# Where a four-byte constant and the identity lie in on-chip memory, in a decoder layer on one core

## The chip, the core and the metric

The kernel runs on one of the eight cores of a Trainium2 chip, as one launch. A core has a matrix engine (TensorE, "PE" in the profile, with its weight loads as a row of their own, "PEld"), two engines for elementwise work (VectorE, "DVE"; ScalarE, "ACT"), GpSimd ("POOL") and SyncE ("SP"), which here only issues transfers, and 16 DMA engines. Engines compute on an on-chip memory of 128 partitions; a tile takes the same range of bytes in each partition, so its place is one byte offset. Matmul results go to a second memory, PSUM.

The metric is the device time of one execution in microseconds (us), as a median of several runs.

## The reference

One layer of a hybrid decoder on 512 tokens of 1024 channels, with one layer of weights. Cut to what is computed:

```python
u = _rmsnorm(h, norm1_g[l])
proj = u @ w_in[l]
a_glu, q, k, v, r, g_low, gate_a, gate_b = _split_cols(proj)

c = a_glu[..., :CONV_CH] * jax.nn.sigmoid(a_glu[..., CONV_CH:])
c = _causal_dwconv(c, conv_dw_w[l], conv_dw_b[l])              # 31 taps
c = jax.nn.silu(_layernorm(c, conv_ln_g[l], conv_ln_b[l]))
y_conv = c @ w_conv_out[l]

gk = jax.nn.log_sigmoid((g_low @ w_gate_up[l] + b_gate[l])) / GATE_NORMALIZER
o = _gla_chunked(qh, kh, vh, gkh)                              # 4 heads, chunks of 64
o = o * lax.rsqrt(jnp.mean(o * o, axis=-1, keepdims=True) + EPS) * gla_norm_g[l]
o = o.reshape(bsz, seq, GLA_VDIM) * jax.nn.silu(r)
y_gla = o @ w_gla_out[l]

merged = jax.nn.sigmoid(gate_a) * y_conv + jax.nn.sigmoid(gate_b) * y_gla
h = h + merged @ w_o[l]

u2 = _rmsnorm(h, norm2_g[l])
z = _causal_dwconv(u2 @ w_ffn_up[l], ffn_dw_w[l], ffn_dw_b[l])  # 3 taps
h = h + (jax.nn.silu(z[..., :FFN_DIM]) * z[..., FFN_DIM:]) @ w_ffn_down[l]
return _rmsnorm(h, final_g)
```

## The kernel before

**Products.** Each fp32 matrix is held as two parts in the type fp32r, a high part (a rounded copy, made by ScalarE) and a low part (the rest, made by VectorE or by a transfer that adds). A product is three matmuls into one PSUM bank: low x high, high x low, high x high. That is `mm3` (lines 554, 555 and 556), and nearly all matmuls of the trace carry these lines. A matmul names a stationary operand, which a weight load brings into the array, and a moving operand of 512 or 256 columns. Some large products are done with seven block products in the place of eight, for which sums of blocks are made first; these have 256 columns, or 512.

**Stages.** In order of time: normalisation and the value projection; the GLU, the convolution's taps on VectorE and the attention's heads beside the input projection; the output gate's projection w_r (about 255 to 280 us), the merge gates with w_gla and w_conv (to about 427 us), w_o with the second norm, and four groups of up-projection and down-projection. Weights are loaded by SyncE's queue into `raw`, split into `whi` and `wlo`, four buffers each, a few tiles ahead of their use.

**What meets in a matmul.** Activations of the input and up-projection are in `u` (uh, ul). In w_conv the stationary operand is whi or wlo and the moving one `ch` (high part) or `c` (low part). In w_r the stationary operand is a slice of u or of sums of it (`hq` in the heap, `sumsq` in the pool late), and the moving one whi or wlo. In the merge gates sums of u move (`hq`, `sumsq`, `c`), in the up-projection `xq`, `usq`, `gainq` and `btmpq`, 256 columns wide. In a row of the profile "mm<-ch,wlo" names the bank and the two operands.

**Places.** Tiles are given places in the order in which they are made, each padded to 32 bytes. Pools made on the left begin at the low end, one behind the other: const, weights, acts, temps, then heap and conv (later ffn). Pools made with "right" come from the high end: edge, and over time gla, late, r, conv_hi, residual. Ahead of const lie 1,024 bytes for descriptors and four small constants of 32 bytes. Three pads in `PADS` shift what comes behind them. The offsets in the compiled program before:

| tile | offset in bytes | modulo 512 |
|---|---|---|
| (pad of 416) | 1,152 | 128 |
| ident, the 128x128 identity for transposes | 1,568 | 32 |
| pp, per-channel parameters | 2,080 | 32 |
| ones, mhalf | 3,904 and 4,416 | 320 |
| eps, four bytes, the bias of one square root in the layer norm (`ln_var`) | 4,448 | 352 |
| shares, run64, keep | 4,480, 4,992, 6,016 | 384 |
| gains | 6,144 | 0 |
| raw, whi, wlo (four each) | from 6,176 on | 32 |
| u (uh, ul; also sums) | from 55,328 on | 32 |
| gain, x and what shares their buffers (gainq, xq, oa) | from 88,096 on | 32 |
| tmp, btmp (also btmpq) | from 107,680 on | 160 |
| heap (h, hq), conv (c), ffn (usq and others) | from 124,704 on | 288 |
| right side: ch, r, sumsq, hres, rx, gate_up, att, q, k, state | from 199,680 on | 0 |

Of the kernel before, what the change touches and what calls it, by code (L numbers as in the profile page):

```python
# [10 lines left out]
F32 = mybir.dt.float32  # L11
# [7 lines left out]
P = 128  # L19
# [35 lines left out]
WARM = (6, 1)  # L55
MID = 4
EARLY = 2
PADS = (416, 992, 768)
ET = mybir.EngineType
SEVEN = {"w_o": KT // 2, "w_down": FT // 2, "w_r": KT // 2}  # L60

# [40 lines left out]
def trunk_layer(ctx: ExitStack, tc: tile.TileContext, a: dict, out: bass.AP):  # L102
    nc = tc.nc

    def pool(name, bufs, space=None):
        kw = {"space": space} if space is not None else {}
        return ctx.enter_context(tc.tile_pool(name=name, bufs=bufs, **kw))
# [7 lines left out]
    cp = pool("const", 1)  # L115
# [13 lines left out]
    def nm(s):  # L129
        return f"{s}_{next(names)}"  # L130
# [30 lines left out]
    for i, part in enumerate((cp, edge)):  # L161
        part.tile([P, PADS[i] // 4], F32, name=nm("pad"))


    ident = cp.tile([P, P], F32, name="ident")
    make_identity(nc, ident)
    pp = cp.tile([P, PP_N], F32, name="pp")
    gate_up = gp.tile([P, HEADS * DK], F32R, name="gate_up")
    ones = cp.tile([P, P], F32, name="ones")
    mhalf = cp.tile([P, NT], F32, name="mhalf")  # L170
    eps = cp.tile([P, 1], F32, name="eps")
    shares = cp.tile([P, P], F32R, name="shares")
    run64 = cp.tile([P, T], BF16, name="run64")
    keep = cp.tile([P, P], U8, name="keep")
# [2 lines left out]
    def load_consts():  # L177
        tc.keep_in_program_order(nc.sync.dma_start(pp, a["pp"]))
        nc.gpsimd.memset(shares.bitcast(F32), -1.0 / D)
        nc.gpsimd.memset(run64, 1.0)  # L180
        nc.gpsimd.memset(run64[:, 0:T:64], 0.0)

        kf = tmp(P)
        nc.gpsimd.memset(kf, 1.0)
        nc.gpsimd.affine_select(
            kf, kf, pattern=[[1, P]], compare_op=ALU.is_ge, fill=0.0, base=0, channel_multiplier=-1
        )
        nc.gpsimd.tensor_copy(keep, kf)
        nc.gpsimd.memset(att, 0.0)
# [661 lines left out]
    start.__exit__(None, None, None)  # L851
    tp.tile([P, PADS[2] // 4], F32, name=nm("pad"))
    load_consts()
# [1205 lines left out]
```

## Time and profile before

| | |
|---|---|
| median of 3 runs | 815.84 us (815.72 to 816.29) |
| profiled execution | 815.9 us |
| its span, first to last instruction | 814.2 us |
| granted TensorE clock, mean | 0.999 |
| busy: ScalarE, GpSimd | 494.9 us (61%), 188.5 us (23%) |
| moved by DMA | 115.71 MB, mean 142 GB/s |

The profile is of one execution. "Busy" is the time in which an engine has an instruction under way; as matmuls overlap and their ends are modelled, a row's duration is longer than the distance from one matmul to the next, which is read from the starts in the timeline. A row of groups gives line, engine, operation, result<-operands, shape, count, busy time, mean ns, and the idle time ahead of it. The chain of work is followed back from the last instruction to what released each step.

### The profile page before, as it was taken

How to read it: one execution, taken by the hardware profiler on the slowest of the kernel's cores; microseconds unless marked ns; L12 is line 12 of the kernel's file. 1: busy time of each engine (PE TensorE's matmuls, PEld its weight loads, DVE VectorE, ACT ScalarE, POOL GpSimd, SP SyncE). 2: the span in 40 equal slices, each digit the busy share in tenths (PEclk: the TensorE clock that was granted, in tenths of full speed). 3: DMA queues.
4: the chain of work that ended last, by engine and by line, in shares of the span. 5: the costliest groups of instructions: out<-in, count | busy, mean ns of one | idle time of the engine just before them, and what ended most of it. 6: DMA issues, size and time to landing. Idle time of an engine off the chain costs nothing.

```text
span 814.2 us, 11423 instructions
## 1 busy us (share of the span) xinstructions
PE 806.4 (99%) x4185; PEld 689.9 (85%) x4185; DVE 708.0 (87%) x1120; ACT 494.9 (61%) x761; POOL 188.5 (23%) x166
## 2 busy tenths in 40 slices
PE   9999999999999999999999999999999999999997
PEld 7888888788888798989888898898889988899885
DVE  6779999998998898786679899979966999789996
ACT  6667788677556785593434655556445563466655
POOL 2025433332204222022001100320133310612010
PEclk9999999999999999999999999999999999999999
DMA  9488858745832443432458513146632446334662
GB/s 334 150 195 174 197 159 173 164 114 129 197 85 83 148 125 104 146 113 96 164 126 205 187 60 122 52 155 156 148 128 87 141 118 167 106 104 158 178 130 105
DMA packets 41385, 115.71 MB, mean 142 GB/s; under 512 B 7960, under 2 KB 13216, under 8 KB 41328
## 3 DMA queue, kind: packets, MB, share of 16 engines
q1 hardware_dynamic: 33968, 89.01, 32.0%
q0 software_dynamic: 7200, 25.69, 18.2%
q8 instruction: 33, 0.54, 0.3%
q14 instruction: 24, 0.20, 0.1%
q10 hardware_dynamic: 160, 0.27, 0.1%
HBM read 110.76 MB, written 3.15 MB: 140 GB/s over the span
## 4 chain that ended last, share of the span: by engine, by line
PE 84%; DVE 14%; issue 1%; ACT 1%; DVEq 0%; ACTq 0%
PE mm L554 20%; PE mm L555 20%; PE mm L556 20%; DVE c L916 5%; PE cv L555 4%; PE cv L554 4%; PE cv L556 4%; DVE aside L916 3%; PE ax L556 2%; PE ax L555 2%; PE ax L554 2%; PE mm L772 1%; PE ax L1232 1%; PE ax L1234 1%; DVE wlo L437 1%
## 5 line engine op out<-in xcount | busy, mean ns | idle before, releaser
L554 PE MATMUL mm<-uh,wlo 128*128 128x512 f32 (+1 forms) x532 | 193.8, 364 | 0.3 <-DVE wlo L477 0.3
L555 PE MATMUL mm<-ul,whi 128*128 128x512 f32 (+1 forms) x532 | 191.6, 360 | 0.0
L556 PE MATMUL mm<-uh,whi 128*128 128x512 f32 (+1 forms) x532 | 191.5, 360 | 0.0
L437 DVE TENSOR_TENSOR wlo<-raw,whi 128x1024 fp32r<-128x1024 f32 x82 | 97.8, 1198 | 29.6 <-ACT whi L435 25.9
L405 POOL TENSOR_TENSOR raw<-raw,raw 128x512 f32<-128x512 f32 x39 | 60.6, 1554 | 241.0 <-DVE wlo L437 134.3
L554 PEld LDWEIGHTS mm<-uh,wlo 128*128 128x128 f32 x532 | 100.5, 189 | 15.8 <-DVE wlo L477 0.7
L556 PEld LDWEIGHTS mm<-uh,whi 128*128 128x128 f32 x532 | 100.4, 189 | 15.4
L555 PEld LDWEIGHTS mm<-ul,whi 128*128 128x128 f32 x532 | 100.5, 189 | 14.7
L435 ACT CAST whi<-raw 128x1024 fp32r<-128x1024 f32 x82 | 78.9, 965 | 36.9 <-PE mm L556 15.1
L468 ACT CAST whi<-raw 128x1024 fp32r<-128x1024 f32 x80 | 83.5, 1047 | 27.5 <-PE mm L556 13.1
L477 DVE TENSOR_TENSOR wlo<-raw,whi 128x1024 fp32r<-128x1024 f32 x50 | 64.7, 1299 | 7.2 <-ACT whi L468 7.1
L435 ACT CAST whi<-kept 128x1024 fp32r<-128x1024 f32 (+1 forms) x40 | 40.1, 1008 | 33.7 <-DVE kept L381 17.5
L437 DVE TENSOR_TENSOR wlo<-kept,whi 128x1024 fp32r<-128x1024 f32 (+1 forms) x40 | 48.3, 1211 | 5.5 <-ACT whi L435 5.4
L916 DVE SCALAR_TENSOR_TENSOR aside<-cv,pp,aside 128x255 f32<-128x255 f32 (+6 forms) x112 | 52.0, 465 | 0.0
L916 DVE SCALAR_TENSOR_TENSOR c<-aside,btmp,c 128x247 f32<-128x247 f32 (+13 forms) x93 | 52.0, 565 | 0.0
L916 DVE SCALAR_TENSOR_TENSOR c<-cv,pp,c 128x247 f32<-128x247 f32 (+13 forms) x93 | 43.1, 463 | 1.4 <-ACT c L912 1.4
L470 ACT ACTIVATE wlo<-raw 128x1024 fp32r<-128x1024 f32 x28 | 29.4, 1059 | 19.1 <-PE mm L554 19.1
L1770 DVE SCALAR_TENSOR_TENSOR tmp<-mm,pp,tmp 128x511 f32<-128x511 f32 (+1 forms) x42 | 31.2, 742 | 3.5 <-ACT tmp L1767 3.5
L1388 ACT COPY tmp<-mm 128x256 f32<-128x256 f32 x38 | 14.0, 368 | 30.3 <-PE mm L556 29.7
L1541 DVE TENSOR_TENSOR hres<-hres,mm 128x512 f32<-128x512 f32 (+1 forms) x37 | 24.6, 674 | 4.3 <-PE mm L556 2.5
L1770 DVE SCALAR_TENSOR_TENSOR tmp<-tmp,pp,tmp 128x511 f32<-128x511 f32 (+1 forms) x32 | 27.8, 888 | 0.4
L555 PE MATMUL cv<-ul,whi 128*128 128x512 f32 (+1 forms) x72 | 25.6, 356 | 0.0
(517 smaller groups left out, 2087.8 us busy)
## 6 DMA issues: line engine op xcount, KB each, us to landing
raw<-in_w_up_dram SPq DMA_DIRECT2D x44, 512.0 KB, 3.3
raw<-in_w_glu_dram SPq DMA_DIRECT2D x16, 512.0 KB, 4.9
raw<-in_w_down_dram SPq DMA_DIRECT2D x16, 512.0 KB, 4.5
wlo<-in_w_glu_dram POOLq DMA_DIRECT2D x12, 512.0 KB, 7.1
kept<-in_w_down_dram POOLq DMA_DIRECT2D x9, 512.0 KB, 5.3
raw<-in_w_v_dram SPq DMA_DIRECT2D x8, 512.0 KB, 6.4
raw<-in_w_qk_dram SPq DMA_DIRECT2D x8, 512.0 KB, 6.1
raw<-in_w_gb_dram SPq DMA_DIRECT2D x8, 512.0 KB, 4.4
```

Source lines behind the costliest of these rows:

```text
L405: work = nc.gpsimd.tensor_tensor(out, x, y, ALU.add)
L435: nc.scalar.copy(hi, raw)
L437: two_low[:] = [nc.vector.tensor_tensor(lo, raw, hi.bitcast(F32), ALU.subtract)]
L468: nc.scalar.copy(hi, raw)
L470: pace[0] = nc.scalar.mul(lo, raw, -1.0)
L477: pace[0] = nc.vector.tensor_tensor(lo, raw, hi.bitcast(F32), ALU.subtract)
L554: nc.tensor.matmul(acc, ll, rh, start=first, stop=False, **kw)
L555: nc.tensor.matmul(acc, lh, rl, start=False, stop=False, **kw)
L556: nc.tensor.matmul(acc, lh, rh, start=False, stop=last, **kw)
L916: nc.vector.scalar_tensor_tensor(out[:, j:], x[:, : half_t - j], w, out[:, j:], ALU.mult, ALU.add)
L1541: done = nc.vector.tensor_tensor(hres[t, n][:, c], hres[t, n][:, c], acc[:, c], op)
L1770: nc.vector.scalar_tensor_tensor(z[:, s:], acc[:, : T - s], w[j], z[:, s:], ALU.mult, ALU.add)
```

## The change

The pad at the head of const is 384 bytes instead of 416, and eps is made directly behind ident instead of behind mhalf:

```diff
-PADS = (416, 992, 768)
+PADS = (384, 992, 768)
...
     ident = cp.tile([P, P], F32, name="ident")
+    eps = cp.tile([P, 1], F32, name="eps")
     make_identity(nc, ident)
     pp = cp.tile([P, PP_N], F32, name="pp")
     gate_up = gp.tile([P, HEADS * DK], F32R, name="gate_up")
     ones = cp.tile([P, P], F32, name="ones")
     mhalf = cp.tile([P, NT], F32, name="mhalf")
-    eps = cp.tile([P, 1], F32, name="eps")
     shares = cp.tile([P, P], F32R, name="shares")
```

By the rule of places, ident goes to 1,536, a multiple of 512, and eps to 2,048, with its 32 bytes up to 2,080; pp, ones and mhalf stay. As no 32 bytes are taken behind mhalf any more, shares and every left-side tile behind it lie 32 bytes lower: where they would lie without eps. The right side stays. The instruction that fills eps stays where it was in the program.

## The prediction

> **What bounds the kernel now.** I read the page first, then busy time by stretches, then the chain of work that ended last, and then, because the change moves nothing but places in memory, the timeline of TensorE with an eye on which places its operands have. The page:
>
> ```profile
> span 814.2 us, 11423 instructions
> ...
> PE 806.4 (99%) x4185; PEld 689.9 (85%) x4185; DVE 708.0 (87%) x1120; ACT 494.9 (61%) x761; POOL 188.5 (23%) x166
> ```
>
> TensorE is busy for 806.4 of 814.2 us. The weight loads (PEld, 689.9 us) run beside the matmuls, so both read the on-chip memory at the same time. Two stretches that matter below, with their columns in the order PE, PEld, DVE, ACT, POOL, granted clock, DMA share, GB/s:
>
> ```profile
> 32.00:132.00 100.00, 99.75 (x441) 82.24 (x440) 90.31 (x203) 77.23 (x121) 35.16 (x33) 1.00 0.76 186
> 360.00:424.00 64.00, 64.00 (x359) 55.53 (x358) 45.93 (x64) 31.05 (x47) 9.01 (x7) 1.00 0.43 128
> ```
>
> The clock is granted in full, and from 360 to 424 us TensorE has no gap at all while VectorE rests for 18 of 64 us. The chain of work there:
>
> ```profile
> by line: PE mm L555 24.9%; PE mm L556 24.8%; PE mm L554 24.8%; PE cv L554 8.6%; PE cv L556 8.6%; PE cv L555 8.6%
> ```
>
> It is TensorE alone: whatever a matmul of this stretch gets shorter by, the kernel gets shorter by. A busy TensorE does not say how fast it goes, though. For that I take the start of one matmul to the start of the next from the timeline. First the input projection, where the moving operand (u) and the stationary one (whi, wlo) both lie 32 bytes past a multiple of 512:
>
> ```profile
> 90.00 0.39 PE L554 MATMUL mm<-uh,wlo 128*128 128x512 f32 x1
> ...
> 91.36 0.39 PE L554 MATMUL mm<-uh,wlo 128*128 128x512 f32 x1
> ```
>
> Six matmuls in 1.36 us are 226.7 ns each. Now the convolution's output projection, w_conv. Its weights lie at 32 as before, but its activations lie at 0 (ch, on the right side of memory) and at 288 (c), all modulo 512:
>
> ```profile
> 408.44 0.40 PE L554 MATMUL mm<-ch,wlo 128*128 128x512 f32 x1
> ...
> 410.54 0.40 PE L554 MATMUL mm<-ch,wlo 128*128 128x512 f32 x1
> ```
>
> Nine matmuls in 2.10 us are 233.3 ns each, 6.6 ns more for the same shape. The output gate's projection, w_r, has the roles turned round: its stationary tiles (sumsq, right side) lie at 0 and its moving weights at 32.
>
> ```profile
> 268.01 0.39 PE L554 MATMUL mm<-whi,sumsq 128*128 128x512 f32 x1
> ...
> 272.21 0.39 PE L554 MATMUL mm<-whi,sumsq 128*128 128x512 f32 x1
> ```
>
> Eighteen in 4.20 us are 233.3 ns again. So before the change there are two paces for one shape, and the slow one stands where left-side and right-side tiles meet in a matmul.
>
> **The change part by part.** It adds, removes and reorders no instruction, wait or transfer; every queue issues the same list. It moves ident from 32 to 0 and eps from behind mhalf to behind ident. Since eps no longer takes 32 bytes behind mhalf, every left-side tile made after it (the constants shares, run64, keep and gains, all weights, activations, temporaries, heap) lies 32 bytes lower. The right side (hres, r, ch, sumsq, q, k, state, att) and pp, ones and mhalf stay. Modulo 512, weights and u go from 32 to 0, heap and c from 288 to 256, tmp and btmp from 160 to 128. The differences among left-side tiles stay; those between left and right change by 32, and w_conv and w_r come to the differences 0 and 256. The trace has a fast case for both: u against whi above (0), and a heap tile at 288 against weights at 32 (256):
>
> ```profile
> 306.06 0.39 PE L554 MATMUL mm<-h,wlo 128*128 128x512 f32 x1
> ...
> 307.42 0.39 PE L554 MATMUL mm<-h,wlo 128*128 128x512 f32 x1
> ```
>
> Six in 1.36 us, 226.7 ns. **First term, w_conv.** Two of the rows of the tile ch (counts, then min/median/max of one in ns; the two banks are mm and cv):
>
> ```profile
> L556 PE MATMUL mm<-ch,whi x48: 390/397/397, 365.2 to 426.4; 128*128 128x512 f32 x48
> L554 PE MATMUL cv<-ch,wlo x16: 392/396/400, 376.1 to 403.5; 128*128 128x512 f32 x16
> ```
>
> 48 and 16 in every product, and three products (L554, L555 with c, L556): 192 matmuls x 6.6 ns = 1.27 us, all on the chain.
>
> **Second term, w_r.** The 18 matmuls up to 272.2 us lie on the chain: 18 x 6.6 ns = 0.12 us. Behind them the chain leaves TensorE; one of its pieces is
>
> ```profile
> 275.84 0.68 DVE r L1598
> ```
>
> Up to about 288 us it runs over ScalarE and VectorE. The further 34 matmuls at this pace (0.22 us) I cost at nothing, as those engines are then what is late; 0.22 us is the other end.
>
> **Third term, 256 columns: a small loss.** Here unlike places are not slower. Both operands at 32:
>
> ```profile
> 482.02 0.28 PE L554 MATMUL mm<-uh,wlo 128*128 128x256 f32 x1
> ...
> 485.26 0.28 PE L554 MATMUL mm<-uh,wlo 128*128 128x256 f32 x1
> ```
>
> The moving operand at 0, the weights at 32:
>
> ```profile
> 374.63 0.28 PE L554 MATMUL mm<-sumsq,wlo 128*128 128x256 f32 x1
> ...
> 376.05 0.39 PE L554 MATMUL cv<-ch,wlo 128*128 128x512 f32 x1
> ```
>
> The moving operand at 160 (and in every third matmul usq, at 288), the weights at 32:
>
> ```profile
> 554.62 0.28 PE L554 MATMUL mm<-btmpq,wlo 128*128 128x256 f32 x1
> ...
> 555.33 0.28 PE L554 MATMUL mm<-btmpq,wlo 128*128 128x256 f32 x1
> ```
>
> 27 in 3.24 us are 120.0 ns, 12 in 1.42 us are 118.3, and 6 in 0.71 us are 118.3. The rows of the tile sumsq count 100 such matmuls, 28 in each of the two largest groups, the rest in groups of 12 and 8:
>
> ```profile
> L554 PE MATMUL mm<-sumsq,wlo x28: 280/282/364, 292.4 to 396.9; 128*128 128x256 f32 x28
> L556 PE MATMUL mm<-sumsq,whi x28: 276/282/285, 292.7 to 397.1; 128*128 128x256 f32 x28
> ```
>
> They go to 120.0: 100 x 1.7 ns = 0.17 us lost. btmp keeps its difference of 128 and its pace. That row also says what the fast state hangs on: 160 and 32 differ by a multiple of 64 and still do not run at 120.0, while 288 and 32 do. So I take the difference modulo 256 as what counts.
>
> **What costs nothing.** VectorE takes the same for a result on the right side (sums, offset 0) as for one on the left (c, 288); the groups by shape:
>
> ```profile
> L1682 DVE TENSOR_TENSOR sums<-tmp,sums 128x512 fp32r<-128x512 f32 x8 | 5.4, 688 | 0.0
> L1053 DVE TENSOR_TENSOR c<-ax,c 128x512 f32<-128x512 f32 x8 | 5.3, 683 | 0.0
> ```
>
> A transfer of w_r takes 6.6 us from issue to landing in a tile at 32 (raw) and 5.7 us in one at 0 (rx):
>
> ```profile
> raw<-in_w_r_dram SPq DMA_DIRECT2D x6, 512.0 KB, 6.6
> ```
>
> ```profile
> rx<-in_w_r_dram SPq DMA_DIRECT2D x1, 512.0 KB, 5.7
> ```
>
> The second is a single transfer, and the chain of the stretch above holds no DMA. I take nothing; a gain could show only in the first 32 us, and I leave 0.3 us for it. The plain fp32 matmuls of the attention run alike with 288 against 0 (h, att) and with both operands at 0 (state, q):
>
> ```profile
> L1232 PE MATMUL ax<-h,att x32: 378/379/483, 154.4 to 239.9; 128*128 128x256 f32 x32
> ```
>
> ```profile
> L1234 PE MATMUL ax<-state,q x24: 379/379/483, 155.5 to 240.3; 128*128 128x256 f32 x24
> ```
>
> 379 ns each. So ident's move should not be felt by the transposes, which are plain fp32 too.
>
> **Sum:** 1.27 + 0.12 - 0.17 = 1.22 us. The profiled execution took 815.9 us around its span of 814.2; the median shown is 815.84, so the two stand within 0.1 us. 815.9 - 1.2 = 814.7, or 814.6 from the median. I forecast **814.6**. Its own range is 814.1 (all of w_r counts, no loss, a little from the start) to 815.2 (half of it is given back to VectorE later).
>
> [...]
>
> **The rivals.** *Nothing changes* (815.9): the slow pace belongs to the right side's tiles themselves, high in memory, and not to a difference of places. For it: ch and sumsq are both up there. Against it: btmpq lies in the middle of the left side and leaves the pace of 120.0 as sumsq does. [...]
>
> *Slower*: a tile that starts on a multiple of 64 is the cause by itself. Every 233.3 above has an operand at 0, and no row shows a 512-column pair of this type with both there. After the change all weights lie at 0 and all u with them. By shape, the groups of this type count 2,694 matmuls of 512 columns, some 250 of them slow already (the largest is the input's and the up-projection's, on three lines):
>
> ```profile
> L554 PE MATMUL mm<-uh,wlo 128*128 128x512 f32 x384 | 151.8, 395 | 0.3 <-DVE wlo L477 0.3
> ```
>
> 2,440 x 6.6 ns = 16 us, less 1 to 2 us on the 256-column ones: about 830. It decides from the first matmuls behind 36 us on. Against it: btmpq at 160 shows that the difference matters without any operand on a multiple of 64.
>
> *Much faster*: between 512 and 256 columns 226.7 - 120.0 = 106.7 ns, so 512 columns stream in 213.4 and 13.3 ns are fixed. Were a part of these due to tiles that start inside a line of memory, half of it gone would be 2,694 x 6.7 ns = 18 us at most, some of it held back by VectorE, which is busy for 90.31 of 100 us between 32 and 132. About 803. Nothing in the trace speaks for it but that no such pair is seen.
>
> **How the numbers follow.** A measurement of this kernel tells 0.2% (1.6 us) from no change; that puts the border of "faster" at 814.2, just inside the forecast's range. Forecast 0.65, of which 0.20 falls under 814.2 and 0.45 over it; nothing changes 0.16; slower 0.09; much faster 0.10. So faster 0.20 + 0.10 = 0.30, same 0.45 + 0.16 = 0.61, slower 0.09. The range holds the forecast and the case of no change, each with its spread: 813.8 to 816.3, with about 0.2 left outside.
>
> **What would show it.** Right: the nine matmuls of w_conv that took 2.10 us take 2.04, the eighteen of w_r 4.08, u against whi stays at 1.36 for six, and w_conv's modelled duration falls from 397 to 389 ns. btmpq stays at 118.3, sumsq in 256 columns goes to 120.0. Wrong in its first step: w_conv stays at 233.3. Wrong in its assumption that pairs at 0 behave as pairs at 32: six of u against whi take 1.40, or 1.32. Wrong in its chain: w_conv is faster and a new gap stands behind 424 us.

## The result and the profile after

The median of 22 executions of the changed kernel is 814.61 us (813.91 to 815.14), against 815.84 us (815.32 to 816.29) of 22 of the kernel before: a ratio of 0.9985, with a 95% interval of 0.998 to 0.9991. That is 0.7 to 1.6 us less, and all of the interval lies on the side of less time. The profiled execution took 814.97 us around a span of 813.3; before it was 815.9 around 814.2. The order of the instructions is the same on each engine.

The page of the kernel after, its first lines:

```profile
span 813.3 us, 11423 instructions
...
PE 804.9 (99%) x4185; PEld 689.4 (85%) x4185; DVE 706.6 (87%) x1120; ACT 495.0 (61%) x761; POOL 188.0 (23%) x166
```

The instruction counts are those of before, and TensorE's busy time is 1.5 us shorter. The busy times by stretches, in the stretch that was TensorE's alone (PE, PEld, DVE, ACT, POOL, granted clock, DMA share, GB/s), and then the chain of waits there:

```profile
360.00:424.00 64.00, 64.00 (x363) 56.31 (x362) 46.21 (x65) 31.47 (x48) 9.03 (x7) 1.00 0.43 128
```

```profile
by line: PE mm L555 25.0%; PE mm L554 25.0%; PE mm L556 24.9%; PE cv L554 8.5%; PE cv L555 8.5%; PE cv L556 8.4%
```

TensorE still has no gap, under the same full clock, but four matmuls more fit into the 64 us: 363 where there were 359. So they run closer together. The timeline of TensorE, w_conv first:

```profile
408.07 0.39 PE L554 MATMUL mm<-ch,wlo 128*128 128x512 f32 x1
...
410.11 0.39 PE L554 MATMUL mm<-ch,wlo 128*128 128x512 f32 x1
```

Nine in 2.04 us, 226.7 ns each where there were 233.3. Then w_r:

```profile
268.08 0.39 PE L554 MATMUL mm<-whi,sumsq 128*128 128x512 f32 x1
...
272.16 0.39 PE L554 MATMUL mm<-whi,sumsq 128*128 128x512 f32 x1
```

Eighteen in 4.08 us, 226.7 ns. And u against the weights, with both operands now on a multiple of 512, as a group by shape (its busy time, then the mean of one):

```profile
L554 PE MATMUL mm<-uh,wlo 128*128 128x512 f32 x384 | 151.8, 395 | 0.0
```

151.8 us and 395 ns, as before. The 256-column matmuls of the merge gates, the timeline again:

```profile
374.58 0.28 PE L554 MATMUL mm<-sumsq,wlo 128*128 128x256 f32 x1
...
376.02 0.40 PE L554 MATMUL cv<-ch,wlo 128*128 128x512 f32 x1
```

Twelve in 1.44 us, 120.0 ns where there were 118.3. The six of btmpq still take 0.71 us. Two of the waits of TensorE that are new are for transfers in the first 25 us (0.3 and 0.2 us). The third lies behind w_r:

```profile
PE cv L554 <- DVE r L1598: 0.3, 1, 0.3
```

It is the output gate's VectorE step, for which TensorE now waits 0.3 us: w_r's later matmuls end earlier, and what follows is hardly earlier.

**Where the difference lies.** Both executions can be cut at the same matmuls. Before, the timeline of w_conv has its first matmul, the first of the next shape, the start of its last long run, and the first matmul behind it:

```profile
364.75 0.40 PE L554 MATMUL mm<-ch,wlo 128*128 128x512 f32 x1
...
367.55 0.28 PE L554 MATMUL mm<-hq,wlo 128*128 128x256 f32 x1
...
401.44 0.40 PE L554 MATMUL cv<-ch,wlo 128*128 128x512 f32 x1
...
426.64 0.40 PE L554 MATMUL cv<-whi,h 128*128 128x512 f32 x1
```

The same after:

```profile
364.78 0.40 PE L554 MATMUL mm<-ch,wlo 128*128 128x512 f32 x1
...
367.53 0.28 PE L554 MATMUL mm<-hq,wlo 128*128 128x256 f32 x1
...
401.24 0.40 PE L554 MATMUL cv<-ch,wlo 128*128 128x512 f32 x1
...
425.75 0.39 PE L554 MATMUL cv<-whi,h 128*128 128x512 f32 x1
```

From its first matmul to the first behind it the product takes 61.89 us before and 60.97 after. These 0.92 us are the 0.9 by which the spans differ. At 364.8 us the two executions stand 0.03 us apart, since what w_r gained is given back by then. Of the product's 192 matmuls 108 are in the run from 401 us on, 25.20 us before and 24.51 after (0.69 us, 6.4 ns each). The other 84 are seven groups of twelve, each between steps of 256 columns: 2.78 to 2.80 us a group before, 19.54 in all, and 2.75 us each after, 19.25 in all (0.29 us, 3.5 ns each). The rest of the stretch, its 256-column steps, got 0.06 us longer.

Twelve at 226.7 ns would be 2.72 us, and twelve at 233.3 would be 2.80. The groups were a little shorter than the one before and are a little longer than the other after, and so they gain half as much as the long run; where the fast pace was missing is shown below, with the step of the prediction that overlooked it.

### The profile page after: what moved, and what is told of

Its sections match the earlier page's. It is cut to its first block, busy times and chain, and to the rows that moved or that the text cites. A ratio compares the mean times of both kernels' runs of the same rounds, so it can differ in the third digit from the quotient of the medians.

```text
span 813.3 us, 11423 instructions
## 1 busy us (share of the span) xinstructions
PE 804.9 (99%) x4185; PEld 689.4 (85%) x4185; DVE 706.6 (87%) x1120; ACT 495.0 (61%) x761; POOL 188.0 (23%) x166
## 4 chain that ended last, share of the span: by engine, by line
PE 84%; DVE 13%; issue 1%; DMA 1%; ACT 1%; SPq 0%; DVEq 0%; ACTq 0%
PE mm L555 19%; PE mm L554 19%; PE mm L556 19%; DVE c L916 5%; PE cv L555 4%; PE cv L554 4%; PE cv L556 4%; DVE aside L916 3%; PE ax L556 2%; PE ax L555 2%; PE ax L554 2%; PE mm L772 2%; DMA raw<-in_w_v_dram 1%; DVE wlo L437 1%; PE ax L1232 1%
```

## The experiments

**The theory** is the prediction's: what counts is the difference of the two operands' byte offsets, modulo 256; equal is fast for 512 columns and slow for 256. Its rivals: that eps or ident matter by themselves, that multiples of 512 do, that tiles high in memory are slow, or that the distance counts modulo 64. In the rows of a tile below, the three numbers behind the count are min, median and max of one in ns, followed by the first and the last start.

**eps moved, the left side left where it was.**

```diff
-PADS = (384, 992, 768)
+PADS = (416, 992, 768)
```

> eps stays behind ident as in the change, but the pad is 416 again, so that ident lies at 32 and all left-side tiles from raw on lie where they lay before (32, 160 and 288 modulo 512), while the right side stays at 0. Theory (the difference of the places of the two operands of a matmul sets its pace): w_conv and w_r run at 233.3 ns again, and the time is that of before, 815.8 +- 0.4 us. Rival (the places of eps or ident themselves matter): about 814.6 us, as after the change.

815.79 us against 815.74 of the kernel before (ratio 1.0001, 0.9992 to 1.001). The tile ch, first in the kernel before, then in this one:

```profile
L554 PE MATMUL mm<-ch,wlo x48: 397/397/400, 364.8 to 425.9; 128*128 128x512 f32 x48
```

```profile
L554 PE MATMUL mm<-ch,wlo x48: 397/397/400, 364.5 to 425.7; 128*128 128x512 f32 x48
```

397 ns and 61.2 us from first to last, as before the change (61.1). Where eps lies is worth nothing that can be told; ident is back at 32 here, so that it could matter is excluded only together with the next runs.

**The kernel before, with its right side 32 bytes off.** ident, eps, the weights and u stay where they were, off the multiples of 512; the right side goes from 0 to 32, as the left side is.

```diff
-PADS = (416, 992, 768)
+PADS = (416, 960, 768)
```

> The kernel before with the right side moved instead of the left: the pad at the high end is 960 bytes, so that ch, sumsq, hres and the other right-side tiles lie at 32 modulo 512, as weights and u do; ident, eps and the left side are as before. Theory (difference of places): w_conv and w_r at 226.7 ns, 256-column sumsq at 120.0, and 814.6 +- 0.4 us, the gain of the change without the change. Rival (tiles high in memory are slow): 815.8 us and 233.3 ns. Rival (multiples of 512 are what helps): 815.8 us.

814.74 us against 815.74 (0.9987, 0.9978 to 0.9996).

```profile
L554 PE MATMUL mm<-ch,wlo x48: 389/389/396, 364.4 to 424.6; 128*128 128x512 f32 x48
```

The gain of the change without the change: 60.2 us from first to last. So no place matters by itself, neither ident's nor a multiple of 512, and ch still lies high in memory. The rival by which nothing happens, as the right side's tiles are slow where they are, falls.

**The changed kernel with its left side 64 bytes up.**

```diff
-PADS = (384, 992, 768)
+PADS = (448, 992, 768)
```

> The change with a pad of 448 instead of 384: the left side lies 64 bytes higher (weights and u at 64, heap at 320 modulo 512), the right side stays at 0, so left and right differ by 64. Theory with a difference modulo 256: w_conv and w_r leave 226.7 ns, the time goes back towards 815.8 us. Theory with a difference modulo 64: 226.7 ns stays and the time is 814.6 us.

815.68 us against 815.74 (0.9999, 0.999 to 1.0007).

```profile
L554 PE MATMUL mm<-ch,wlo x48: 397/398/403, 364.0 to 425.3; 128*128 128x512 f32 x48
```

Slow again, so the distance doesn't count modulo 64.

**A sweep by itself.** The layer is left out: the kernel loads numbers, rounds them, and runs 35 stretches of 48 matmuls of this type that differ only in where the stationary (st) and the moving operand (mv) begin in their tiles, both of which lie on a multiple of 512. ScalarE has rounded them by 15.5 us; from then on no other compute engine has work.

```python
for n, (s, m, cols) in enumerate(SWEEP):
    ...
    for k in range(EACH):
        w = st[:, s // 4 + (k % 24) * P : s // 4 + (k % 24 + 1) * P]
        x = mv[:, m // 4 + (k % 8) * T : m // 4 + (k % 8) * T + cols]
        nc.tensor.matmul(acc[:, :cols], w, x, start=k % 24 == 0, stop=k % 24 == 23)
```

> Leaves the whole layer out: 32 stretches of 48 matmuls of 512 or 256 columns in fp32r with nothing else running, a weight load for each, with the moving operand 0 to 480 bytes past a multiple of 512 and the stationary one at 0, 32, 64, 128 or 256. Its time says nothing of the layer; what counts is the distance from one matmul to the next in each stretch. Theory (difference modulo 256): 226.7 ns at differences 0 and 256, about 233 at 32, 64, 96, 128, 160, 192 and 224; 256 columns 120.0 at 0 and 256 and about 118.3 at 32, 64, 128 and 160. Theory (difference modulo 64): 226.7 at every multiple of 64. Rival (something else that runs beside w_conv and w_r slows them, not the places): one pace for all. Differences under 32 bytes are shown by no run yet.

It took 365.12 us in all. The timeline has one row for each stretch (start, duration; the result's name tells the offsets, some cut at their front, and "half" is 256 columns). The pace is the distance to the next row's start by 48:

```profile
78.62 11.16 PE L118 MATMUL mvsixtyfour<-mv,st 128*128 128x512 f32 x48
89.62 11.37 PE L118 MATMUL mvninetysix<-mv,st 128*128 128x512 f32 x48
...
145.65 11.05 PE L118 MATMUL mvtwofiftysix<-mv,st 128*128 128x512 f32 x48
156.54 11.37 PE L118 MATMUL mvtwoeightyeight<-mv,st 128*128 128x512 f32 x48
...
289.44 11.36 PE L118 MATMUL thirtytwomvonesixty<-mv,st 128*128 128x512 f32 x48
300.64 11.07 PE L118 MATMUL twomvtwoeightyeight<-mv,st 128*128 128x512 f32 x48
311.56 11.07 PE L118 MATMUL mvzero<-mv,st 128*128 128x512 f32 x48
...
322.46 5.92 PE L118 MATMUL mvzerohalf<-mv,st 128*128 128x256 f32 x48
328.21 5.82 PE L118 MATMUL mvthirtytwohalf<-mv,st 128*128 128x256 f32 x48
```

A moving operand 256 bytes off takes 10.89 us to the next stretch, 226.9 ns a matmul. With the stationary operand at 32, a moving one at 160 takes 11.20 us (233.3) and one at 288 takes 10.92 (227.5). With 256 columns equal places take 5.75 us (119.8). All stretches from 15.5 us on worked out so:

| columns | stationary, moving offset | ns a matmul |
|---|---|---|
| 512 | 0, 0 (twice) and 0, 256 and 256, 0 | 226.9 to 227.1 |
| 512 | 0, 0 at the very start (42 matmuls) | 230.0 |
| 512 | 32, 32 and 64, 64 and 32, 288 | 227.3 to 227.5 |
| 512 | 0, 64 and 0, 320 | 229.2 |
| 512 | 64, 0 | 233.1 |
| 512 | 0 and 4, 8 and 16 (43, 43 and 47 matmuls) | 235.3, 233.0 and 231.7 |
| 512 | 0 and 32, 48, 96, 128, 160, 192, 224, 288, 384, 448 or 480 | 232.5 to 234.2 |
| 512 | 32, 0 and 128, 0 and 32, 160 | 232.5 to 233.3 |
| 256 | 0, 0 and 0, 256 | 119.8 |
| 256 | 0 and 32, 64, 128 or 160 | 117.3 to 118.8 |

So in a stretch of pairs that are all alike the difference modulo 256 decides at the places tried, and the sign turns round with 256 columns. No VectorE work and no wait is needed for it: the kernel has none of the first, and from 15.5 us on its rows show no idle time of TensorE. One thing is not as the theory has it: a moving operand 64 bytes ahead of the stationary one loses only 2.3 ns, one 64 bytes behind it loses 6.2.

**The activations 32 bytes off.** In the changed kernel every tile from u on goes up by 32 bytes; the weights stay.

```diff
+    up.tile([P, 8], F32, name=nm("pad"))
```

> The change with 32 bytes put between the weights and the activations: raw, whi and wlo stay at 0 modulo 512, while u, x, gain, tmp, heap and conv lie 32 bytes higher (32, 32, 32, 160, 288, 288); the right side stays at 0. Now nearly every product has operands at unlike places. Theory (difference modulo 256): some 2,570 matmuls of 512 columns go from 226.7 to 233.3 ns, 16.9 us, of which about 0.7 us fall where TensorE is not what is late; some 1,100 matmuls of 256 columns go from 120.0 to about 117.8, 2.4 us won; together 814.6 + 13.8 = about 828 us (826 to 830). Rival (only products with a right-side tile can be slow): 814.6 us.

824.32 us against 815.57 (1.0106, 1.0092 to 1.012), the largest effect of all and the right sign, but 9.7 us above the change (824.32 - 814.61) where 828 would have been 13.4. The busy times by stretches, first of the changed kernel, then of this one:

```profile
36.00:132.00 96.00, 96.00 (x426) 79.47 (x425) 86.31 (x200) 74.91 (x117) 35.12 (x33) 1.00 0.77 187
132.00:264.00 132.00, 131.88 (x603) 109.06 (x601) 125.35 (x249) 87.20 (x159) 40.54 (x35) 1.00 0.56 133
```

```profile
36.00:132.00 96.00, 96.00 (x414) 77.15 (x413) 84.44 (x194) 72.73 (x112) 35.10 (x32) 1.00 0.76 184
132.00:264.00 132.00, 132.00 (x597) 108.21 (x596) 123.47 (x252) 87.36 (x160) 42.42 (x35) 1.00 0.56 133
```

In the first stretch 2.8% fewer matmuls fit (414 for 426), which is 233.3 over 226.7. In the second only 1.0% fewer do (597 for 603); VectorE is busy for 125 of its 132 us there, and a part of the matmuls is the attention's. Compared start by start with the changed kernel, the 2,585 fp32r matmuls of 512 columns (all but one ahead of a long wait) lose 13.9 us together, 5.4 ns each and not 6.6; the 1,259 of 256 columns give 2.9 back, plain fp32 and waits 1.5.

**Only w_r taken back.** The sums go 32 bytes off on the right, and with them rx, r and hres, which lie in the same part; a pad behind them puts ch back on its multiple of 512.

```diff
+    shift = ctx.enter_context(tc.tile_pool(name="shift", bufs=1, side="right"))
+    shift.tile([P, 8], F32, name=nm("pad"))
...
-        conv_hi, chp = scoped("conv_hi", 1, "right")
+        conv_hi, gap = scoped("gap", 1, "right")
+        gap.tile([P, 120], F32, name=nm("pad"))
+        chp = conv_hi.enter_context(tc.tile_pool(name="conv_hi", bufs=1, side="right"))
```

> The change with the pool of the late sums (sumsq) and what lies under it at 480 modulo 512, and ch at 0 as in the change: the w_r part of the gain alone is taken back. w_r's 52 matmuls go to 233.3 ns, the 100 of sumsq with 256 columns to about 117.8. If w_r's matmuls count on the chain only up to 272 us, as forecast: +0.12 - 0.2, no difference to the change, 814.5 us. If all of them count: +0.34 - 0.2, 814.8 us. Both lie within what a measurement tells; the trace decides by the paces and by where the chain leaves TensorE.

814.44 us against 815.57 (0.9987, 0.9978 to 0.9996). The tile sumsq:

```profile
L555 PE MATMUL mm<-wlo,sumsq x12: 393/396/397, 267.7 to 278.2; 128*128 128x512 f32 x12
```

w_r is at its old pace and the gain is all there: w_r is worth less than this can tell.

**Only w_conv taken back.** ch goes 32 bytes off; the sums stay.

```diff
-        conv_hi, chp = scoped("conv_hi", 1, "right")
+        conv_hi, gap = scoped("gap", 1, "right")
+        gap.tile([P, 8], F32, name=nm("pad"))
+        chp = conv_hi.enter_context(tc.tile_pool(name="conv_hi", bufs=1, side="right"))
```

> The change with ch alone at 480 modulo 512: the w_conv part of the gain alone is taken back. If that part is 1.27 us, as forecast: 815.8 us, with w_conv at 233.3 ns and w_r at 226.7. If the gain came from elsewhere: 814.6 us.

815.63 us against 815.57 (1.0, 0.9991 to 1.0008).

```profile
L554 PE MATMUL mm<-ch,wlo x48: 397/397/400, 364.6 to 425.9; 128*128 128x512 f32 x48
```

61.3 us from first to last, and all of the gain is gone. The gain is w_conv's.

**The 256-column sums unlike their weights.** If unlike places are faster for 256 columns, the sums of the up-projection should lie off the weights. First with pads at two places, of 480 and 160 bytes:

```diff
-PADS = (384, 992, 768)
+PADS = (384, 992, 800)
...
+    tp.tile([P, 120], F32, name=nm("pad"))
...
+            fp.tile([P, 40], F32, name=nm("pad"))
```

> The change with the sums that are used only with 256 columns moved away from the weights on purpose: btmp from 128 to 160 and usq from 256 to 416 modulo 512 (416 and 160 are the same modulo 256), all else as in the change. By the stretches with 256 columns (120.0 ns at a difference of 0, 117.3 at 160), 160 matmuls win 1 to 2.7 ns: 0.2 to 0.4 us, 814.3 us. Rival (the paces with 256 columns don't carry over to three products in turn): 814.6 us.

816.48 us against 815.57 (1.001, 1.0002 to 1.0019): slower. The tile sh:

```profile
L555 PE MATMUL mm<-wlo,sh x59: 392/399/399, 573.7 to 797.8; 128*128 128x512 f32 x59
```

The pad had moved the down-projection's activations as well, ah, al, sh and sl, to 416 modulo 512, and with them 318 matmuls of 512 columns to the slow pace: 318 x 6.6 ns = 2.1 us at most. In the trace what lies behind w_conv takes 1.9 us more than in the changed kernel (389.4 us for 387.5). A second kernel made the 160-byte pad directly before the first of the sums, so that the activations stay:

```diff
+        gap = []
+
+        def us():
+            if not gap:
+                gap.append(fp.tile([P, 40], F32, name=nm("pad")))
+            return us_at()
```

> As the kernel with the sums moved away from the weights, but with the 160 bytes put right before usq, so that the down-projection's operands (ah, al, sh, sl) stay at 256 modulo 512; there they had come to 416 with usq, and 318 matmuls of 512 columns had weights at 0 against them. If these 318 matmuls made that kernel slower (318 x 6.6 ns = 2.1 us): 814.4 to 814.6 us here. If moving btmp and usq did it: 816.5 us again. Whether 160 matmuls of 256 columns win anything shows in their pace, not in the time: 0.2 us at most.

814.34 us against 815.65 (0.9983, 0.9974 to 0.9992). The same row is fast again, at a median of 389 ns:

```profile
L555 PE MATMUL mm<-wlo,sh x59: 389/389/462, 573.0 to 795.1; 128*128 128x512 f32 x59
```

Beside it, on the same chip, ran the changed kernel itself:

> The changed kernel itself once more, beside the others of this call: 814.6 us, 226.7 ns in w_conv's long run and in w_r. It says how far two profiled executions of one kernel lie apart, which the single profile of after leaves open (its span was 0.9 us under that of before, the medians 1.2 us).

814.22 us (0.9983, 0.9974 to 0.9992). The two times don't differ, and no version here is faster than the change by them. The traces do differ: what lies behind w_conv takes 387.2 us with the sums unlike their weights, against 387.5 in both profiles of the changed kernel. So the gain from 256 columns is about the 0.2 to 0.4 us that was expected, and the time of one execution varies by more than that.

## Why the prediction was right, and where its sum was not

**What bounds the kernel, and the two paces: right.** TensorE alone ends last from 360 to 424 us, and 233.3 became 226.7 ns in w_conv and w_r. Undoing w_conv's part alone takes the whole gain away.

**The difference modulo 256: right where all pairs of a run are alike, with an exception.** It was chosen from three rows of the profile before (differences of 0, 256 and 128). The sweep shows the same for its 26 pairs of places with 512 columns, but for the 64 bytes that cost 2.3 ns one way and 6.2 the other, and 16 bytes, which cost 4.8.

**It is not the whole rule, and the prediction did not keep to it.** A third of w_conv's matmuls are c against whi. Before, they lay at 288 and 32, a difference of 256, which is the prediction's own fast case (h against wlo). By the rule these 64 of the 192 had nothing to gain, and the first term would have been 128 x 6.6 ns = 0.84 us. They were slow all the same (231 ns from the start of one to the next in the long run, by the trace), and became faster (before, then after):

```profile
L555 PE MATMUL mm<-c,whi 128*128 128x512 f32 x48 | 18.9, 393 | 0.0
```

```profile
L555 PE MATMUL mm<-c,whi 128*128 128x512 f32 x48 | 18.7, 390 | 0.0
```

If only a matmul's own two operands counted, the long run would have gained 72 x 6.6 ns = 0.48 us; it gained 0.69. The run with the activations 32 bytes off shows the same from the other side. There ch and the weights both lie at 0, and only c is unlike its weights, yet the same 108 matmuls take 25.02 us (the kernel's lines count one further there):

```profile
405.28 0.40 PE L555 MATMUL cv<-ch,wlo 128*128 128x512 f32 x1
...
430.30 0.40 PE L555 MATMUL cv<-whi,h 128*128 128x512 f32 x1
```

That is 0.51 us over the changed kernel, where 36 x 6.6 ns are 0.24. So the pairs of neighbouring matmuls count too. Which neighbour, and which of its operands, stays open, as the pairs of each stretch of the sweep are all alike. That 192 matmuls at 6.6 ns was nearly right for the long run is owed to the measured pace, a mean over nine matmuls of all three kinds, and not to the rule.

**First term, w_conv, 1.27 us: mis-sized.** This is the step that failed. It took 192 matmuls at 6.6 ns; the profiled pair shows 0.69 + 0.29 = 0.98 us. The long run did as forecast (108 x 6.6 = 0.71). The seven groups of twelve gave 0.29 in the place of 84 x 6.6 = 0.55, as the first matmuls behind a step of 256 columns don't run at the fast pace: in each group of the changed kernel the first six take 1.39 us, where six at 226.7 ns are 1.36. The trace of before shows this already, in a pair at equal places, u against the weights behind a step of 256 columns:

```profile
485.62 0.40 PE L554 MATMUL mm<-uh,wlo 128*128 128x512 f32 x1
...
487.01 0.39 PE L554 MATMUL mm<-uh,wlo 128*128 128x512 f32 x1
...
488.37 0.39 PE L554 MATMUL mm<-uh,wlo 128*128 128x512 f32 x1
```

The first six take 1.39 us (231.7 ns each), the next six 1.36 (226.7). The prediction read the fast pace from the middle of a long run and gave it to every matmul.

**Second term, w_r: right in the main.** 4.20 us became 4.08. The later matmuls (30 by the trace, where the prediction counts 34) did end earlier: the last of them starts at 278.73 us, which was 278.97. But the new wait for VectorE takes nearly all of that back, and 3.5 us later the lead is 0.07 us (282.26 for 282.33). Taken back alone, w_r changes no time.

**Third term, the 256 columns: right.** Twelve take 1.44 us for 1.42, and the steps inside w_conv's stretch grew by 0.06 us. Between 282.3 us and w_conv's first matmul the changed kernel turns from 0.07 us ahead to 0.03 behind, and by the starts in the traces most of these 0.10 us lie in the 256-column steps on sumsq and hq. Together they are 0.16 us, for a forecast of 0.17.

**The sum.** The profiled pair differs by 0.9 us and the medians by 1.23, with an interval of 0.7 to 1.6. The forecast of 814.6 against 814.61 is closer than its terms deserve: with w_conv at its measured size they give 0.98 + 0.12 - 0.17 = 0.93 us, or 814.9. The interval holds both, and one execution differs from the next by more than that (813.91 to 815.14 in the changed kernel). Whether the 0.3 us between are chance stays open; nothing in the trace behind 426 us shows them. The second profile of the changed kernel says where executions differ: its product takes the same 60.97 us and what follows 387.5, but its span is 1.0 us shorter (812.3), of which 0.7 us are there at TensorE's 43rd matmul (11.33 us for 12.05), where the first transfers land.

**What costs nothing: right as far as seen.** eps and ident gave nothing that can be told (815.79 us against 815.74 with eps moved alone), and the gain without any change on the left was the same within what can be told (1.0 us for 1.2), so transfers into tiles on a multiple of 512 brought nothing either.

**The rivals.** *Nothing changes* fell with the right side moved by 32 bytes (814.74 us against 815.74). With the layer left out, the sweep has 226.9 and 233.3 ns for one shape by the two operands' places alone. What in the chip makes this difference no run shows. *Slower* fell in u against the weights with both at 0: 151.8 us as before, 226.9 ns in the sweep. What that rival described is real where the places are unlike: 9.7 us in the run with the activations 32 bytes off. *Much faster* fell in the same rows: a pair at 0 is as fast as a pair at 32, within 0.6 ns.

**The activations' run was mis-sized by the same error.** 6.6 ns for each of the 512-column matmuls was too much; 5.4 ns is what they lost. Outside w_conv, and but for 39 on sumsq, whose places stay, the 361 among the first six behind a change of shape lost 1.7 ns each, as they were slow already, and the 1,993 further on 6.2.

## What to carry to other kernels

Where TensorE has no gap, read its pace from the starts in the timeline, shape by shape, and if one shape shows two paces, set the byte offsets of the stationary and the moving operand side by side, over all the matmuls that take turns, before looking for a wait: here equal places modulo 256 throughout were worth 6.6 ns of 233 in a 512-column fp32r matmul. A small tile made in between moves what is placed behind it: here a constant of four bytes and a pad brought 1.2 us by the medians without one instruction changed. And a pad that mends one pair can break another, as with the down-projection (816.48 us with it moved, 814.34 without). And count such a gain by runs of matmuls of one shape, not by all matmuls of the product.

## What the runs showed of the hardware

- Four bytes are enough: in the sweep a moving operand 4 bytes off its partner's place took 235.3 ns a matmul (a stretch of 43), 16 bytes off 231.7, 32 bytes off 233.5, against 226.9.
- Unlike pairs slow their neighbours: with one matmul in three unlike, w_conv's long run took 231.7 ns a matmul (25.02 us for 108), with two in three 233.3 (25.20 us), about as much as with all unlike in the sweep (233.5 at 32 bytes). If each pair set its own pace alone, 226.7 ns and 6.6 more where unlike would give 228.9 and 231.1.
- The effect isn't symmetric at 64 bytes (229.2 ns with the moving operand ahead, 233.1 with the stationary one). At 128 the two take 233.3 and 232.5, and at 256 both take 226.9.
- With 256 columns the sign turns: 119.8 ns for equal places, 117.3 to 118.8 for unlike ones.
- The fast pace is not there at once. Behind a step of 256 columns the first six matmuls of u against the weights took 1.39 us (231.7 ns each) even at equal places, the next six 1.36 (226.7). What sets this is open.
